# Expert look-ups of a PEER layer summed along contiguous positions, with wide products for every u item

## Chip, core and metric

One core of a Trainium2 chip runs the whole program in one launch. The metric is the device time of a launch in microseconds. TensorE is called PE here, VectorE DVE, ScalarE ACT, GpSimd POOL and SyncE SP, as in the profile.

## What is computed

256 tokens of width 1024 pass through two residual layers. Layer 0 mixes with a gated causal convolution, layer 1 with causal attention of 16 heads (256 tokens are one MoBA block, so it is plain causal attention). Each is followed by a PEER expert mixer, which is most of the work:

```python
q = (xc @ w_q).reshape(PEER_CHUNK, PEER_HEADS, 2, PEER_HALF)
s1 = jnp.einsum('thd,nd->thn', q[:, :, 0], sub_k1)      # 128 keys per half
s2 = jnp.einsum('thd,nd->thn', q[:, :, 1], sub_k2)
v1, i1 = lax.top_k(s1, 16); v2, i2 = lax.top_k(s2, 16)
cand = v1[..., :, None] + v2[..., None, :]              # 16 x 16 sums
cidx = i1[..., :, None] * 128 + i2[..., None, :]
top_s, top_pos = lax.top_k(cand, 16)
e_idx = jnp.take_along_axis(cidx, top_pos, axis=-1)     # the look-up
g = jax.nn.softmax(top_s, axis=-1)
a = jax.nn.gelu(jnp.einsum('td,thkd->thk', xc, u_emb[e_idx]))
out = jnp.einsum('thk,thkd->td', g * a, v_emb[e_idx])
```

There are 8 heads and 128 x 128 experts a layer.

## The kernel before, in words

**No gather.** The kernel multiplies all tokens with all 16384 rows of u and of v. The activations of all experts for all tokens lie in one large tensor, `big`, and those experts that a token did not choose are made zero by a product with one-hot rows. So a PEER layer is a u stage (128 items of 128 experts, 512 KB each), in which `A[:, k]` (a part of `big`) gets the gelu of item k, and a v stage of 128 items.

**Two parts of each number.** Every matrix is split into an upper part HI (fp32r) and the rest LO = value - HI, and a product is upper x upper + upper x lower + lower x upper. For an item of u the chain is: SP's queue loads RAW; DVE transposes RAW into TR (line 157); ACT writes HI (line 171); POOL writes LO in two halves (line 176); PE multiplies. Each of these has three buffers. `next_item` (line 221) puts the instructions of an item into every engine's queue in this order: the transposes for three items ahead, the splits for two ahead, the matmuls, then side work, then what was left for last.

**Narrow and wide products of u.** `products` calls `upper` for the eight 128-row blocks and then `lower` for the eight. `u_bank(k)` decides the form. The first 16 items of a layer (WIDE = 16) are narrow: a PSUM region of 256 columns, into which `upper` puts two matmuls of 256 columns (lines 967 and 968) and `lower` one (line 971). Gelu then reads two such items from the bank (line 1126). The later ones are wide: one matmul of 512 columns in `upper` (line 965), for the token's upper and lower parts side by side, so that a bank of 512 columns holds one item, and its two halves still have to be added. After each odd item ACT copies the second halves of two banks to A (line 1144), DVE adds the first halves (`both`, line 1134), and two items later ACT takes the gelu in place. Four banks serve in turn, so the matmuls of a pair of items wait for the addition of the pair before the last one.

**Side work.** Everything else of the layer (scores, top 16, look-ups, one-hot rows) goes into a queue `side` as pieces with a cost in microseconds, written by hand. `run_side` is called after the matmuls of each item with a budget (1.62 for an item of u); it issues pieces in order while their costs fit the credit, and a `pause` ends the item's share and sets the credit to zero. Pieces issued through `add` carry line 215 in the profile, those of `words` line 1020, of `fold` line 1029. DVE works through its queue in order; transposes, side pieces and additions stand in one line.

**The look-up.** For each half of the tokens (i = 0, 1) the top 16 of 65 candidate sums give positions, of which four bits name an entry of the second list and a table of steps the entry of the first. `hits` are one-hot rows, 16 heads-and-sides x 16 positions x 16 picks in float16, laid out with positions outside and picks inside; they are multiplied with the values (each value twice in the bank, so that pairs can be read), and then summed over positions with three folds (halves of the tile added to each other, both operands in SBUF) and a last addition. The subtraction of the largest score, `gg = ts - ts[0]`, is an operation with both operands in SBUF too. The bank `hi4[3]` holds picks, values and small intermediate numbers.

**The stage before.** In the attention layer `attn_mixer` multiplies the items of q, k and v; lower parts of some of these are POOL's (`on_pool`), in one instruction unless the item is in `halved`. The first two items of v are multiplied together by `next_group`, a bank at a time (lines 565 to 567).

Of the kernel before, what the change touches and what calls it, by code (L numbers as in the profile page):

```python
# [12 lines left out]
F16 = mybir.dt.float16  # L13
BF16 = mybir.dt.bfloat16
I32 = mybir.dt.int32
U32 = mybir.dt.uint32
AF = mybir.ActivationFunctionType
# [16 lines left out]
WIDE = (16, 16)  # L34
# [4 lines left out]
def trunk_kernel(ctx: ExitStack, tc, x, norm_mix, norm_ffn, conv_w_in, conv_w, conv_w_out,  # L39
# [43 lines left out]
    def scratch(off, n):  # L83
        return big[:, off:off + n]
# [610 lines left out]
    def attn_mixer():  # L695
# [131 lines left out]
        for g, banks in ((0, lo4), (1, hi4), (2, lo4)):  # L827
            n = state["use"] - 3 * (g == 0)
            if g == 0:
                on_pool.update(range(n + 15, n + 20))  # L830
                hi_dve.update(range(n + 21, n + 26))
# [75 lines left out]
    def peer(l):  # L907
# [4 lines left out]
        vp = [xbuf[:, 256 * i:256 * i + 256].bitcast(F16).rearrange("p (g a r) -> p g a r", a=16, r=2) for i in range(2)]  # L912
        hot = [scratch(base + 2048 * i, 2048).bitcast(F16).rearrange("p (g a n) -> p g a n", a=16, n=16)
               for i in range(2)]
# [8 lines left out]
        pf = scratch(o + 2176, 128).bitcast(F16).rearrange("p (s h n) -> p s h n", s=2, h=8)  # L923
# [5 lines left out]
        picks = hi4[3][:, 0:128].bitcast(F16).rearrange("p (s h n) -> p s h n", s=2, h=8)  # L929
        values = hi4[3][:, 128:384].bitcast(F16).rearrange("p (g a r) -> p g a r", a=16, r=2)  # L930
# [3 lines left out]
        io16 = scratch(o + 3280, 128).bitcast(F16).rearrange("p (a n) -> p a n", a=16)  # L934
        st16 = scratch(o + 3408, 128).bitcast(F16).rearrange("p (a n) -> p a n", a=16)
# [10 lines left out]
        pool.iota(io16, pattern=[[1, 16], [0, 16]], base=0, channel_multiplier=0,  # L946
                  allow_small_or_imprecise_dtypes=True)
        for a0, n, first, width in ((0, 1, 0, 0), (1, 2, 16, 8), (3, 4, 32, 4), (7, 9, 48, 2)):
            pool.iota(st16[:, a0:a0 + n], pattern=[[width, n], [0, 16]], base=first, channel_multiplier=0,
                      allow_small_or_imprecise_dtypes=True)  # L950
# [71 lines left out]
        def tables(i):  # L1022

            act.activation(vp[i][:, 0:8, 0], if16[:, i, 0, :, 0:1].to_broadcast([128, 8, 2]), AF.Copy)
            act.activation(vp[i][:, 8:16], if16[:, i, 1, :, :, None].to_broadcast([128, 8, 16, 2]), AF.Copy)

        def fold(i, n):
            v = hot[i].rearrange("p g a n -> p g (a n)")
            dve.tensor_tensor(v[:, :, 0:16 * n], v[:, :, 0:16 * n], v[:, :, 16 * n:32 * n], op=OP.add)
# [20 lines left out]
        for i in range(2):  # L1050
            add(0.4, words, room(0, 256), i16[:, i].rearrange("p s h n -> p (s h n)"))
            add(0.3, dve.tensor_copy, if16[:, i].rearrange("p s h n -> p (s h n)"), room(0, 256))
            add(0.4, dve.tensor_tensor, vp[i][:, 0:8, 1:16], if16[:, i, 0, :, 1:16, None].to_broadcast([128, 8, 15, 2]),
                if16[:, i, 0, :, 0:15, None].to_broadcast([128, 8, 15, 2]), op=OP.subtract)
# [10 lines left out]
            add(0.5, dve.tensor_tensor, gg[:, i], ts[:, i], ts[:, i, :, 0:1].to_broadcast([128, 8, 16]),  # L1065
# [7 lines left out]
            add(0.3, dve.tensor_copy, pf.rearrange("p s h n -> p (s h n)"), room(128, 256))  # L1073
            if i:
                add(0.0, act.activation, gg, gg, AF.Exp)
            add(0.3, words, hi4[3][:, 0:128].bitcast(U32), pf.rearrange("p s h n -> p (s h n)").bitcast(U32))
            add(0.4, words, hi4[3][:, 128:384].bitcast(U32), vp[i].rearrange("p g a r -> p (g a r)").bitcast(U32))
            add(1.4, dve.tensor_tensor, hot[i][:, 0:8], picks[:, 0, :, None, :].to_broadcast([128, 8, 16, 16]),
# [6 lines left out]
            for n in (8, 4, 2):  # L1085
                add(0.3 + 0.14 * n, fold, i, n)
# [260 lines left out]
```

## Time and profile before

| | |
|---|---|
| median of 3 runs | 1809.76 us (1808.52 to 1813.9) |
| the profiled execution | 1812.88 us, of which the span is 1811.1 us |
| PE busy | 99% of the span |
| DVE, ACT, POOL busy | 76%, 50%, 39% |
| DMA | 321 MB, 177 GB/s |
| mean granted clock of PE | 0.995 |

The profile is of one execution; the span runs from the first to the last instruction of the program, and the time of the execution is a little longer. Times in rows are in microseconds from the span's start. A row of the timeline has the start, the length, the engine, the line, the operation, output <- inputs, shapes and a count of merged instructions; a bracket holds the idle time before it and what ended it. Consecutive matmuls overlap in these rows, so a period is read from one start to the next. Within layer 0 the u stage lies from about 139 to 500 us, within layer 1 from about 1049 us on; the look-ups of layer 0 lie between 226 and 320 us.

### The profile page before, as it was taken

To read this page: it belongs to the slowest core of one execution; us is meant where nothing else is said; L and a number is where in the kernel's file an instruction comes from. 1 tells how busy PE (TensorE), PEld (TensorE's weight loads), DVE (VectorE), ACT (ScalarE), POOL (GpSimd) and SP (SyncE) were. 2 spreads that over 40 slices of the span, in tenths; PEclk is the share of its full clock that TensorE was granted. 3 is DMA by queue.
4 is the path that set the end of the run, shared out by engine and by line. 5 is a ranking of instruction groups with operands and counts; after the bars stand their busy time and mean duration, and the time that the engine had idled before them with its cause. 6 is when DMAs were issued, how large, how long until landed. Compare 5 with 4: busy or idle time off the path is not lost.

```text
span 1811.1 us, 30954 instructions
## 1 busy us (share of the span) xinstructions
PE 1791.1 (99%) x11217; PEld 1536.6 (85%) x11217; DVE 1370.7 (76%) x2251; ACT 906.8 (50%) x1153; POOL 700.2 (39%) x553
## 2 busy tenths in 40 slices
PE   9999999999999999999999999999999999999998
PEld 8979988888888888888878799888888888888886
DVE  4648899888888887555566488998888898875555
ACT  5455555554554444544454555565455544445443
POOL 1047888888720000000220388988888200000000
PEclk9999999999999999999999999999999999999999
DMA  7566566656556556766562665665565565657664
GB/s 206 157 196 197 167 176 174 187 166 176 171 157 182 168 171 185 228 193 196 172 181 83 174 198 168 182 179 174 172 175 164 158 186 169 176 176 230 193 193 138
DMA packets 204576, 321.06 MB, mean 177 GB/s; under 512 B 26221, under 2 KB 157317, under 8 KB 203910
## 3 DMA queue, kind: packets, MB, share of 16 engines
q1 hardware_dynamic: 202006, 312.33, 58.4%
q10 hardware_dynamic: 2416, 6.75, 1.1%
q8 instruction: 88, 1.44, 0.3%
q14 instruction: 66, 0.54, 0.1%
HBM read 315.83 MB, written 3.15 MB: 176 GB/s over the span
## 4 chain that ended last, share of the span: by engine, by line
PE 87%; DVE 7%; DMA 3%; issue 1%; ACT 1%; POOL 1%; SPq 1%; DVEq 0%; ACTq 0%; POOLq 0%
PE psum L558 40%; PE psum L965 19%; PE psum L971 11%; PE psum L1189 4%; PE psum L545 3%; DVE tr L157 2%; DVE big L215 2%; PE psum L968 2%; PE psum L967 2%; PE psum L591 2%; DMA raw<-in_peer_u_dram 1%; DVE lo L176 1%; PE psum L1003 1%; POOL lo L176 1%; PE psum L567 1%
## 5 line engine op out<-in xcount | busy, mean ns | idle before, releaser
L176 POOL TENSOR_TENSOR lo<-tr,hi 128x512 fp32r<-128x512 f32 x496 | 632.5, 1310 | 120.1 <-ACT hi L171 120.1
L171 ACT ACTIVATE hi<-raw 128x1024 fp32r<-128x1024 f32 x331 | 350.0, 1060 | 452.4 <-PE psum L558 362.7
L176 DVE TENSOR_TENSOR lo<-raw,hi 128x1024 fp32r<-128x1024 f32 x312 | 382.7, 1228 | 253.6 <-ACT hi L171 247.4
L558 PE MATMUL psum<-hi,x 128*128 128x512 f32 x2208 | 553.2, 392 | 0.7 <-ACT hi L171 0.7
L558 PEld LDWEIGHTS psum<-hi,x 128*128 128x128 f32 x2208 | 409.0, 188 | 82.6 <-ACT hi L171 1.1
L965 PE MATMUL psum<-x,hi 128*128 128x512 f32 x1792 | 458.9, 397 | 5.2 <-DVE big L1134 5.2
L965 PEld LDWEIGHTS psum<-x,hi 128*128 128x128 f32 x1792 | 323.2, 190 | 64.6 <-issue 4.2
L157 DVE STREAM_TRANSPOSE tr<-raw 128x1024 f32<-128x1024 f32 x256 | 315.6, 1233 | 43.2 <-DMA raw<-in_peer_u_dram 26.6
L171 ACT ACTIVATE hi<-tr 128x1024 fp32r<-128x1024 f32 x256 | 270.7, 1059 | 144.5 <-DVE tr L157 134.1
L558 PE MATMUL psum<-lo,x 128*128 128x512 f32 x1104 | 295.1, 389 | 0.4 <-POOL lo L176 0.4
L971 PEld LDWEIGHTS psum<-x,lo 128*128 128x128 f32 x2048 | 279.5, 191 | 18.0 <-POOL lo L176 0.2
L176 POOL TENSOR_TENSOR lo<-raw,hi 128x1024 fp32r<-128x1024 f32 (+1 forms) x31 | 58.3, 1904 | 599.7 <-ACT hi L171 558.1
L971 PE MATMUL psum<-x,lo 128*128 128x256 f32 x2048 | 289.2, 283 | 0.0
L558 PEld LDWEIGHTS psum<-lo,x 128*128 128x128 f32 x1104 | 207.1, 188 | 43.8 <-POOL lo L176 0.8
L1144 ACT ACTIVATE big<-psum 128x512 f32<-128x512 f32 x112 | 66.8, 596 | 165.6 <-PE psum L971 165.4
L1289 POOL TENSOR_TENSOR big<-xbuf,big 128x256 f32<-128x256 f32 x2 | 1.4, 732 | 383.4 <-DVE rstd L348 383.4
L1134 DVE TENSOR_TENSOR big<-psum,big 128x512 f32<-128x512 f32 x112 | 77.2, 689 | 72.3 <-ACT big L1144 72.0
L1174 DVE TENSOR_TENSOR xbuf<-psum,eT 128x1536 f16<-128x1536 f16 x128 | 119.8, 936 | 10.2 <-PE psum L1189 10.2
L1196 DVE SCALAR_TENSOR_TENSOR big<-psum,big 128x512 f32<-128x512 f32 x128 | 86.5, 677 | 3.1 <-PE psum L1189 3.1
L1182 DVE TENSOR_TENSOR xbuf<-xbuf,psum 128x1024 f16<-128x1024 f16 x128 | 85.8, 671 | 1.3
L1189 PEld LDWEIGHTS <-xbuf 128*128 128x128 f16 x2048 | 68.5, 97 | 19.5 <-issue 15.7
L1189 PE MATMUL psum<-xbuf 128*128 128x64 f16 x2048 | 83.7, 193 | 0.0
(173 smaller groups left out, 1451.0 us busy)
## 6 DMA issues: line engine op xcount, KB each, us to landing
raw<-in_peer_u_dram SPq DMA_DIRECT2D x1024, 128.0 KB, 2.9
raw<-in_peer_v_dram SPq DMA_DIRECT2D x256, 512.0 KB, 3.7
raw<-in_conv_w_in_dram SPq DMA_DIRECT2D x96, 128.0 KB, 2.7
raw<-in_attn_w_qkv_dram SPq DMA_DIRECT2D x96, 128.0 KB, 2.6
raw<-in_peer_w_q_dram SPq DMA_DIRECT2D x64, 128.0 KB, 3.1
raw<-in_conv_w_out_dram SPq DMA_DIRECT2D x8, 512.0 KB, 3.9
raw<-in_attn_w_o_dram SPq DMA_DIRECT2D x8, 512.0 KB, 3.6
x_dram<-xbuf ACTq DMA_DIRECT2D x2, 1024.0 KB, 4.8
```

The lines of the kernel that those rows point to most:

```text
L157: dve.transpose(TR[m % 3].rearrange("p b (g i) -> p g b i", g=4), RAW[m % 3].rearrange("p (g m) -> p g m", m=256))
L171: act.activation(HI[m % 3], src, AF.Copy)
L176: eng.tensor_sub(LO[m % 3][:, c], src[:, c], HI[m % 3][:, c])
L558: pe.matmul(banks[j], x[:, j // 2 * 128:j // 2 * 128 + 128], w[:, j % 2 * 512:j % 2 * 512 + 512], start=(first and p == 0), stop=(last and ...
L965: pe.matmul(o, w, X2[:, b], start=(b == 0), stop=False, skip_group_check=True)
L971: pe.matmul(o[:, 0:256], lo[:, b * 128:b * 128 + 128], XH[:, b], start=False, stop=(b == 7), skip_group_check=(o.shape[-1] == 512))
L1134: dve.tensor_tensor(a, halves(k, 0), a, op=OP.add)
L1144: act.activation(A[:, k - 1:k + 1], halves(k, 1), AF.Copy)
L1174: dve.tensor_tensor(HOT[s % 2].rearrange("p b (r k) t -> p b r k t", r=3), numbers[:, None, None].to_broadcast([128, TOK // 2, 3, 64, 2]), ...
L1182: dve.tensor_tensor(OHG[s % 2], one_hot[:, None].to_broadcast([128, 2, TOK // 2, 64, 2]), gate_rows[:, s, :, :, None, :].to_broadcast([128 ...
L1189: pe.matmul(o, pairs[:, t // 2, :, t % 2], OHG[s % 2][:, a, t // 2, :, t % 2], start=(a == 0), stop=(a == 1))
L1196: dve.scalar_tensor_tensor(w, banks[s % 3].rearrange("p (t k) -> p k t", k=64), 1.0 / GSC, w, op0=OP.mult, op1=OP.mult)
```

## The change

- `WIDE` goes from 16 to 0 in both layers: all u items are wide.
- The hits are laid out with picks outside and positions inside, so that the sum over the 16 positions runs along contiguous elements; two `tensor_reduce` replace the three folds and the closing addition. Picks lie in the bank twice (pairs), values once.
- The position numbers (`numb`) and the scores for the subtraction are first copied into the bank, so that no operation of the look-up has two operands in SBUF.
- The constant tables are 16 numbers each instead of 256; the table copies are smaller.
- A `pause` goes ahead of the sum of the gates, and some costs are written anew.
- The lower parts of the first two items of v are written in two halves.

```diff
@@ -31,7 +31,7 @@
 NEG = -1.0e30
 TOK = 8
 WARM = 22
-WIDE = (16, 16)
+WIDE = (0, 0)
 HEADS = ((0, 0), (0, 1), (1, 0), (0, 2), (0, 3), (1, 1), (1, 2), (1, 3))
 
 
@@ -828,6 +828,7 @@
             n = state["use"] - 3 * (g == 0)
             if g == 0:
                 on_pool.update(range(n + 15, n + 20))
+                halved.update((n + 16, n + 17))
                 hi_dve.update(range(n + 21, n + 26))
             if g:
                 next_group(qkv_first(banks), None, 2.5 * (g == 1))
@@ -909,8 +910,8 @@
         S = scratch(base, 4096).rearrange("p (b h s n) -> p b h s n", b=2, h=8, s=2)
         qT = scratch(80 * 256, 2048).rearrange("p (h t) -> p h t", t=256)
         qs = scratch(60 * 256, 1024).rearrange("p (t c) -> p t c", t=2)
-        vp = [xbuf[:, 256 * i:256 * i + 256].bitcast(F16).rearrange("p (g a r) -> p g a r", a=16, r=2) for i in range(2)]
-        hot = [scratch(base + 2048 * i, 2048).bitcast(F16).rearrange("p (g a n) -> p g a n", a=16, n=16)
+        vp = [xbuf[:, 128 * i:128 * i + 128].bitcast(F16).rearrange("p (g a) -> p g a", a=16) for i in range(2)]
+        hot = [scratch(base + 2048 * i, 2048).bitcast(F16).rearrange("p (g n a) -> p g n a", a=16, n=16)
                for i in range(2)]
         o = base + 4096
         cand = scratch(o, 8 * 66).rearrange("p (h c) -> p h c", c=66)
@@ -920,19 +921,19 @@
         if16 = scratch(o + 1024, 256).bitcast(F16).rearrange("p (b s h n) -> p b s h n", b=2, h=8, s=2)
         ts = scratch(o + 1280, 256).rearrange("p (b h n) -> p b h n", b=2, h=8)
         tp = scratch(o + 1536, 512).bitcast(U32).rearrange("p (b s h n) -> p b s h n", b=2, s=2, h=8)
-        pf = scratch(o + 2176, 128).bitcast(F16).rearrange("p (s h n) -> p s h n", s=2, h=8)
+        pf = scratch(o + 2048, 256).bitcast(F16).rearrange("p (m r) -> p m r", r=2)
         f15 = scratch(o + 2368, 128).bitcast(U32).rearrange("p (h n) -> p h n", h=8)
         e12 = scratch(o + 2496, 512).rearrange("p (b s n) -> p b s n", b=2, s=2)
         gg = scratch(o + 3008, 256).rearrange("p (b h n) -> p b h n", b=2, h=8)
         gs = scratch(o + 3264, 16).rearrange("p (b h) -> p b h", b=2)
 
-        picks = hi4[3][:, 0:128].bitcast(F16).rearrange("p (s h n) -> p s h n", s=2, h=8)
-        values = hi4[3][:, 128:384].bitcast(F16).rearrange("p (g a r) -> p g a r", a=16, r=2)
+        picks = hi4[3][:, 0:256].bitcast(F16).rearrange("p (s m r) -> p s m r", s=2, r=2)
+        values = hi4[3][:, 256:384].bitcast(F16).rearrange("p (g a) -> p g a", a=16)
         side1 = hi4[3][:, 384:512].rearrange("p (h n) -> p h n", h=8)
         room = lambda a, n: hi4[3][:, a:a + n].bitcast(U32)
         gr = hi4[3][:, 384:400].rearrange("p (b h) -> p b h", b=2)
-        io16 = scratch(o + 3280, 128).bitcast(F16).rearrange("p (a n) -> p a n", a=16)
-        st16 = scratch(o + 3408, 128).bitcast(F16).rearrange("p (a n) -> p a n", a=16)
+        io16 = scratch(o + 3280, 8).bitcast(F16)
+        st16 = scratch(o + 3408, 8).bitcast(F16)
         kbd = scratch(o + 3536, 256)
         kk = scratch(28416, 128)
 
@@ -943,10 +944,9 @@
         V0 = U0 + NK
         on_dve.update(range(V0 - 4, V0))
         act.dma_start(x_dram, xo)
-        pool.iota(io16, pattern=[[1, 16], [0, 16]], base=0, channel_multiplier=0,
-                  allow_small_or_imprecise_dtypes=True)
-        for a0, n, first, width in ((0, 1, 0, 0), (1, 2, 16, 8), (3, 4, 32, 4), (7, 9, 48, 2)):
-            pool.iota(st16[:, a0:a0 + n], pattern=[[width, n], [0, 16]], base=first, channel_multiplier=0,
+        pool.iota(io16, pattern=[[1, 16]], base=0, channel_multiplier=0, allow_small_or_imprecise_dtypes=True)
+        for a0, n, first, width in ((0, 1, 0, 1), (1, 2, 16, 8), (3, 4, 32, 4), (7, 9, 48, 2)):
+            pool.iota(st16[:, a0:a0 + n], pattern=[[width, n]], base=first, channel_multiplier=0,
                       allow_small_or_imprecise_dtypes=True)
         pool.iota(f15, pattern=[[0, 8], [0, 16]], base=15, channel_multiplier=0)
         pool.memset(kbd, 0.0)
@@ -1021,12 +1021,14 @@
 
         def tables(i):
 
-            act.activation(vp[i][:, 0:8, 0], if16[:, i, 0, :, 0:1].to_broadcast([128, 8, 2]), AF.Copy)
-            act.activation(vp[i][:, 8:16], if16[:, i, 1, :, :, None].to_broadcast([128, 8, 16, 2]), AF.Copy)
-
-        def fold(i, n):
-            v = hot[i].rearrange("p g a n -> p g (a n)")
-            dve.tensor_tensor(v[:, :, 0:16 * n], v[:, :, 0:16 * n], v[:, :, 16 * n:32 * n], op=OP.add)
+            act.activation(vp[i][:, 0:8, 0:1], if16[:, i, 0, :, 0:1], AF.Copy)
+            act.activation(vp[i][:, 8:16], if16[:, i, 1], AF.Copy)
+
+        def hits(i, c, ends, op):
+
+            dve.tensor_tensor(hot[i][:, 8 * c:8 * c + 8].rearrange("p h n (a r) -> p (h n) a r", r=2),
+                              picks[:, c, :, None].to_broadcast([128, 128, 8, 2]),
+                              ends.rearrange("p (a r) -> p a r", r=2)[:, None].to_broadcast([128, 128, 8, 2]), op=op)
 
         def ask(h):
             for i in range(2):
@@ -1048,10 +1050,10 @@
                 q_turn(0)
         q_out(1)
         for i in range(2):
-            add(0.4, words, room(0, 256), i16[:, i].rearrange("p s h n -> p (s h n)"))
-            add(0.3, dve.tensor_copy, if16[:, i].rearrange("p s h n -> p (s h n)"), room(0, 256))
-            add(0.4, dve.tensor_tensor, vp[i][:, 0:8, 1:16], if16[:, i, 0, :, 1:16, None].to_broadcast([128, 8, 15, 2]),
-                if16[:, i, 0, :, 0:15, None].to_broadcast([128, 8, 15, 2]), op=OP.subtract)
+            numb = hi4[3][:, 0:256].rearrange("p (s h n) -> p s h n", s=2, h=8)
+            add(0.4, dve.tensor_copy, numb, i16[:, i])
+            add(0.3, dve.tensor_copy, if16[:, i], numb)
+            add(0.4, dve.tensor_tensor, vp[i][:, 0:8, 1:16], numb[:, 0, :, 1:16], if16[:, i, 0, :, 0:15], op=OP.subtract)
             add(0.3, dve.tensor_copy, side1, v16[:, i, :, 1])
             for a0, n, first, width in ((0, 1, 0, 16), (1, 2, 16, 8), (3, 4, 32, 4), (7, 8, 48, 2), (15, 1, 64, 1)):
                 add(0.4, dve.tensor_tensor,
@@ -1062,7 +1064,8 @@
                 topk([(cand[:, h + a, 0:65], ts[:, i, h + a], tp[:, i, 0, h + a]) for a in range(4)], 0.25)
                 if h == 0:
                     add(0.0, tables, i)
-            add(0.5, dve.tensor_tensor, gg[:, i], ts[:, i], ts[:, i, :, 0:1].to_broadcast([128, 8, 16]),
+            add(0.3, dve.tensor_copy, side1, ts[:, i])
+            add(0.3, dve.tensor_tensor, gg[:, i], side1, ts[:, i, :, 0:1].to_broadcast([128, 8, 16]),
                 op=OP.subtract)
             top = tp[:, i, 0].rearrange("p h n -> p (h n)")
             add(0.3, words, room(128, 128), top)
@@ -1070,22 +1073,18 @@
             add(0.3, dve.tensor_tensor, room(0, 128), f15.rearrange("p h n -> p (h n)"), room(0, 128),
                 op=OP.logical_shift_right)
             add(0.3, dve.tensor_tensor, room(256, 128), top, room(0, 128), op=OP.bitwise_and)
-            add(0.3, dve.tensor_copy, pf.rearrange("p s h n -> p (s h n)"), room(128, 256))
+            add(0.6, dve.tensor_copy, pf, room(128, 256)[:, :, None].to_broadcast([128, 256, 2]))
             if i:
                 add(0.0, act.activation, gg, gg, AF.Exp)
-            add(0.3, words, hi4[3][:, 0:128].bitcast(U32), pf.rearrange("p s h n -> p (s h n)").bitcast(U32))
-            add(0.4, words, hi4[3][:, 128:384].bitcast(U32), vp[i].rearrange("p g a r -> p (g a r)").bitcast(U32))
-            add(1.4, dve.tensor_tensor, hot[i][:, 0:8], picks[:, 0, :, None, :].to_broadcast([128, 8, 16, 16]),
-                st16[:, None].to_broadcast([128, 8, 16, 16]), op=OP.is_ge)
-            add(1.4, dve.tensor_tensor, hot[i][:, 8:16], picks[:, 1, :, None, :].to_broadcast([128, 8, 16, 16]),
-                io16[:, None].to_broadcast([128, 8, 16, 16]), op=OP.is_equal)
-            pairs = hot[i].rearrange("p g a (n r) -> p g a n r", r=2)
-            add(2.5, dve.tensor_tensor, pairs, pairs, values[:, :, :, None, :].to_broadcast([128, 16, 16, 8, 2]),
-                op=OP.mult)
-            for n in (8, 4, 2):
-                add(0.3 + 0.14 * n, fold, i, n)
-            add(0.6, dve.tensor_tensor, e12[:, i].rearrange("p s (h n) -> p (s h) n", h=8), hot[i][:, :, 0],
-                hot[i][:, :, 1], op=OP.add)
+            add(0.4, words, room(0, 256), pf.rearrange("p m r -> p (m r)").bitcast(U32))
+            add(0.3, words, room(256, 128), vp[i].rearrange("p g a -> p (g a)").bitcast(U32))
+            add(1.2, hits, i, 0, st16, OP.is_ge)
+            add(1.2, hits, i, 1, io16, OP.is_equal)
+            add(2.3, dve.tensor_tensor, hot[i], hot[i], values[:, :, None].to_broadcast([128, 16, 16, 16]), op=OP.mult)
+            for c in range(2):
+                add(1.7, dve.tensor_reduce, e12[:, i, c].rearrange("p (h n) -> p h n", h=8),
+                    hot[i][:, 8 * c:8 * c + 8], axis=AX.X, op=OP.add)
+        pause()
         add(0.8, dve.tensor_reduce, gs, gg, axis=AX.X, op=OP.add)
         add(0.2, dve.reciprocal, gr, gs)
         add(0.8, dve.tensor_tensor, gg, gg, gr[:, :, :, None].to_broadcast([128, 2, 8, 16]), op=OP.mult)
```

## Rows read from the trace of the kernel before

**Rows 1.** The page: busy time of each engine, and two of its costliest groups.
```profile
PE 1791.1 (99%) x11217; PEld 1536.6 (85%) x11217; DVE 1370.7 (76%) x2251; ACT 906.8 (50%) x1153; POOL 700.2 (39%) x553
...
L176 POOL TENSOR_TENSOR lo<-tr,hi 128x512 fp32r<-128x512 f32 x496 | 632.5, 1310 | 120.1 <-ACT hi L171 120.1
...
L1174 DVE TENSOR_TENSOR xbuf<-psum,eT 128x1536 f16<-128x1536 f16 x128 | 119.8, 936 | 10.2 <-PE psum L1189 10.2
```

**Rows 2.** Waits of PE: total us, times, the longest us.
```profile
PE psum L965 <- DVE big L1134: 5.2, 4, 1.9
```

**Rows 3.** Timeline of PE: first matmuls of two narrow items, then of two wide ones.
```profile
145.67 0.28 PE L967 MATMUL psum<-x,hi 128*128 128x256 f32 x1
...
148.55 0.28 PE L967 MATMUL psum<-x,hi 128*128 128x256 f32 x1
...
281.61 2.00 PE L965 MATMUL psum<-x,hi 128*128 128x512 f32 x8
...
284.40 2.00 PE L965 MATMUL psum<-x,hi 128*128 128x512 f32 x8
```

**Rows 4.** Timeline of PE: u items around the waits, layer 0, then layer 1.
```profile
292.78 2.00 PE L965 MATMUL psum<-x,hi 128*128 128x512 f32 x8
...
296.42 2.08 PE L965 MATMUL psum<-x,hi 128*128 128x512 f32 x8 [0.69 <-DVE big L1134]
...
315.82 3.62 PE L965 MATMUL psum<-x,hi 128*128 128x512 f32 x8 [1.91 <-DVE big L1134]
...
320.23 2.00 PE L965 MATMUL psum<-x,hi 128*128 128x512 f32 x8
...
1225.91 2.73 PE L965 MATMUL psum<-x,hi 128*128 128x512 f32 x8 [1.92 <-DVE big L1134]
```

**Rows 5.** Windows: stretch, us, then busy time of each engine, clock, DMA.
```profile
138.90:189.30 50.40, 50.40 (x409) 49.93 (x408) 42.10 (x168) 25.27 (x31) 41.09 (x34) 1.00 0.64 189
...
190.00:230.00 40.00, 40.00 (x230) 35.13 (x229) 36.13 (x128) 22.30 (x29) 36.09 (x29) 1.00 0.58 170
...
315.80:319.30 3.50, 3.48 (x9) 2.77 (x10) 3.46 (x7) 2.32 (x4) 1.63 (x2) 0.52 0.37 105
```

**Rows 6.** Timeline of DVE in the look-ups of layer 0.
```profile
262.39 2.06 DVE L1029 TENSOR_TENSOR big<-big 128x2048 f16<-128x2048 f16 x1
...
271.80 0.68 DVE L1134 TENSOR_TENSOR big<-psum,big 128x512 f32<-128x512 f32 x1
...
290.93 4.22 DVE L215 TENSOR_TENSOR big<-big 128x128 f32<-128x128 f32 x1
...
295.60 0.68 DVE L1134 TENSOR_TENSOR big<-psum,big 128x512 f32<-128x512 f32 x1
...
310.50 4.57 DVE L1029 TENSOR_TENSOR big<-big 128x2048 f16<-128x2048 f16 x3
315.00 0.68 DVE L1134 TENSOR_TENSOR big<-psum,big 128x512 f32<-128x512 f32 x1
```

**Rows 7.** DVE's groups from 226 to 324 us: count | busy us, mean ns | idle.
```profile
L157 DVE STREAM_TRANSPOSE tr<-raw 128x1024 f32<-128x1024 f32 x33 | 40.7, 1234 | 0.5 <-DMA raw<-in_peer_u_dram 0.5
L1134 DVE TENSOR_TENSOR big<-psum,big 128x512 f32<-128x512 f32 x17 | 11.6, 684 | 3.0 <-ACT big L1144 3.0
...
L215 DVE TENSOR_TENSOR big<-psum,big 128x2048 f16<-128x2048 f16 x4 | 4.7, 1184 | 0.0
L215 DVE TENSOR_TENSOR big<-big,psum 128x4096 f16<-128x4096 f16 x2 | 4.5, 2249 | 0.0
...
L215 DVE TENSOR_TENSOR big<-big,psum 128x128 f32<-128x128 f32 x8 | 1.8, 271 | 0.0
...
L215 DVE TENSOR_REDUCE big<-big 128x16 f32<-128x256 f32 x1 | 0.4, 402 | 0.0
```

**Rows 8.** Timeline around the first two items of v: POOL and PE.
```profile
941.51 4.73 POOL L176 TENSOR_TENSOR lo<-raw,hi 128x1024 fp32r<-128x1024 f32 x2 [1.27 <-ACT hi L171]
...
943.93 0.50 PE L567 MATMUL psum<-lo,x 128*128 128x512 f32 x1 [1.72 <-POOL lo L176]
```

## The prediction

> **What bounds the kernel now.** I read the page's busy times first: TensorE (PE) is busy for 1791.1 us of a span of 1811.1 us [rows 1], so little can be won but what PE waits for, what it does slowly, and the instructions that it need not issue. Then the waits of PE: the largest by far is for line 1134, the DVE addition that empties two PSUM banks of the u stage, 5.2 us in 4 waits [rows 2]. The timeline of PE shows where: two waits in the u stage of each layer, of 0.69 and 1.91 us in layer 0 and as long in layer 1 [rows 4]. After the second wait eight matmuls take 3.62 us where they take 2.00 elsewhere [rows 3, 4], and the granted clock over these 3.5 us is 0.52 [rows 5], so the lower level (1.2 GHz) for nearly all of them: PE had idled for 1.9 us just before. A u item has a period of 2.79 us (281.61 to 284.40) where the products are wide, and of 2.88 us (145.67 to 148.55) in the first 16 items, where they are narrow [rows 3]. From 292.78 to 320.23 lie eight items; 27.45 us less 8 x 2.79 is 5.13 us lost [rows 4]. That is the waits, the slow clock and about 0.9 us of small slips.
>
> Why the addition is late stands in the DVE timeline [rows 6]. Ahead of the first late addition (295.60) lies a subtraction of 128 elements that took 4.22 us; ahead of the second (315.00) lie three folds, 4.57 us together. An operation on 128 elements with one operand in PSUM takes 0.27 us [rows 7]. GpSimd (POOL) meanwhile works nearly without a pause: two lower parts of 1.31 us an item [rows 1], 2.62 of 2.79 us. I read the 4.22 us as a wait for POOL, by an operation that has both operands in SBUF.
>
> The Trainium skill, "SBUF — State Buffer", section "Who interferes with whom", says that a DVE instruction with two SBUF inputs contends with a GpSimd instruction that reads SBUF and that the second one to issue blocks in full, while one with at most one SBUF input, outside the two-port modes, does not contend. By that rule the subtraction costs what rows 7 show for 128 elements; if instead it were slow by itself, the waits would stay, and that is rival 3.
>
> **The change part by part.**
>
> 1. *All u products wide.* Items 0 to 15 of each layer change from 24 matmuls to 16: 2.88 - 2.79 = 0.09 us each, 32 items, **2.9 us**, on PE and so on the path. It adds to DVE, in each layer, 8 of the additions of line 1134 at 0.684 us [rows 7], 5.5 us, and to ACT 8 copies. What hides them: in this stretch ACT is busy 25.27 and DVE 42.10 of 50.40 us [rows 5], so 8.3 us of DVE are idle; with the additions it has 47.6 us of work against 49.0 us that PE will need. Behind an addition in DVE's queue stand the next transpose and the top-16 search; the next pair of items but one waits for the addition. The same mixture (wide products, top-16 searches) already runs from 190 to 230 us: DVE busy 36.13 of 40 us, PE all 40.00 [rows 5]. Bounds: nothing, or all 8.3 us of idle stay idle (47.6 + 8.3 - 49.0 = 6.9 us a layer). I take nothing, because the nearest stretch shows it.
>
> 2. *Subtraction of the largest score.* A copy to the bank and a subtraction with a bank operand, both near 0.27 us, instead of 4.22 us in the second list [rows 6, 7]. **DVE is 3.7 us earlier there.**
>
> 3. *Picks.* The pairs copy writes 512 elements (nearest row: line 1134 with 512, 0.684 us) where it wrote 256: 0.27 us more by the slope in step 5. The words of the picks double, those of the values halve. Together about +0.3 us a list. The first steps (numbers held in the bank) come out even. Table copies on ACT and iotas on POOL shrink; neither is waited for.
>
> 4. *Hits and product.* Same element counts: 2 x 1.184 and 2.249 us [rows 7]. The hits now walk in pairs with one operand repeated; line 1174 does that with 1536 elements in 0.936 us [rows 1], the same rate. So I take no change; the other end, one element at a time, is worked out under rival 2.
>
> 5. *Folds against two sums.* Three folds (4.57 us in list two) and the closing pair addition go; two reductions of 2048 elements come. No row has that. Low end: 1.184 us, the hits' pace. High end: the 0.402 us of a reduction of 256 elements times eight, 3.22 us. I take 2.33: 0.402 plus 1792 elements at (1.234 - 0.684) / 512 = 1.07 ns, the slope between 512 and 1024 elements on DVE [rows 7].
>
> The Trainium skill, "VectorE: DVE Perf Modes", section "Rules for kernel authors", speaks against this step: expect one element at a time from a reduction, the slowest operation of the engine, and restructure. By the page's clock of 0.96 GHz 2048 elements are an estimated 2.1 us plus the start, so it excludes the low end and agrees with 2.33; its warning holds for folds that are not held up, and here they are [rows 6].
>
> 6. *One pause more, other costs.* Adding up the planner's costs against its 1.62 an item: the lists come one item later (after 64 items, not 63), the one-hot products of the first half end at item 124 instead of 123 of 127, before the last item would have to drain them. Price: nothing. More useful: at most one reduction goes into one item, where three folds went into one.
>
> 7. *v's lower parts halved.* PE waits 1.72 us at 943.93 for the second v item's lower part, which POOL began at 941.51 and which takes 2.4 us (4.73 for two) [rows 8]. In halves of 1.31 us the first is there at 942.82, **1.1 us** earlier; the second, at 944.1, is wanted six matmuls after PE starts again, some 1.4 us (an item of 2.79 us holds eight of these and eight of half the width), so in time. POOL's next item comes 0.2 us later, and PE first has the rest of this group to do.
>
> **Do the waits go?** The addition that started at 295.60 let PE start 0.85 us late (295.57, which is 292.78 + 2.79, became 296.42), so its deadline was 294.75; those of the other pairs lie 2 x 2.79 = 5.58 us apart. In the second list DVE is free at 290.93. Four small operations put the first addition at 292.05 (deadline 294.75). From there each pair costs DVE two transposes at some 1.16 us (they overlap a little), the addition at 0.6, and its share of the list: 297.9 (300.3), then with a hit and the product 304.1 (305.9), one reduction 309.3 (311.5), the other and the closing sums 315.2 (317.1). The least spare time is 1.8 us. In the first list a reduction stands where a fold began at 262.39; the addition behind it comes at 264.7 (deadline 266.85), the next, after another reduction and five small steps (1.6 us), at 271.5 (272.43; before it was 271.80, and PE did not wait). Spare 0.9 us. So both waits go, and with no idle PE before it the slow clock goes too: **5.1 us a layer, 10.2 us**; layer 1 is taken like layer 0. Late next is POOL, with 0.17 us to spare an item; it falls behind only if a transpose is late, and DVE's lag shrinks.
>
> Sum: 2.9 + 10.2 + 1.1 = 14.2 us. The profiled execution took 1812.88 us (span 1811.1): 1798.7 after. The median shown, 1809.76, is 3.1 us below it, with runs from 1808.52 to 1813.9; 14.2 off it is 1795.6. If the faster runs were those in which the clock did not fall (2 x 1.6 us), they have less to gain, if they differ by something else, as much. I put the forecast between: **1797.2 us**.
>
> **Rivals.**
>
> Rival 1, *the reductions are long*: at 3.22 us the second addition of the first list starts at 273.2, 0.8 us past its deadline; with a fall of the clock behind it (1.6 us) that is 2.4 a layer, 1802.0 us. For: no row of this size. Against: the slope, and that the wait of 0.69 us drew no slow clock (the item after it took 2.08 us).
>
> Rival 2, *slower than before*: the pair form loses double rate, hits 2.3 us each, product 4.4. First list: the addition after the product starts 2.3 us past its deadline, the next another 1.3; second list: 2.6. With a slow stretch of 1.6 us after each: 11 us a layer, 22 us, 1819.2 us. It decides from a product of about 4 us on. Against: line 1174 [rows 1].
>
> Rival 3, *the bank does not help*: DVE's small operations still wait 4 us for POOL; only 2.9 + 1.1 us are won, 1797.2 + 10.2 = 1807.4 us, no measurable change. For: only one such operation shows the extreme. Against: operations with a bank operand show steady times [rows 7].
>
> Rival 4, *the first 16 items become DVE's*: up to 6.9 us a layer, 1811 us at worst; half of that, 1804, is likelier. Against: rows 5.
>
> **How the numbers follow.** The forecast has 0.74, rival 1 0.11, rival 2 0.04, rival 3 0.05, rival 4 0.06. A difference of under 0.3% (5.4 us, about the spread of the runs shown) can hardly be told from none: faster means under 1804.3, slower over 1815.2. The forecast and rival 1 are faster, as is a piece of rival 4: 0.86. Rival 3 and the rest of 4: 0.10. Rival 2: 0.04. The range reaches down to 1792.5 (3 us of scatter below the median's own 1795.6) and up to 1803.5, which takes in rival 1 and leaves out rivals 2, 3 and most of 4.
>
> **What would show it.** Right: no wait of PE for line 1134, granted clock 1.0 through both u stages, 2.79 us an item from the first on, the subtraction under 0.3 us, reductions near 2.3 us, PE's wait at the second v item under 0.7 us. Wrong: an addition of line 1134 that PE still waits for, a product over 4 us, items over 2.85 us among the first 16, or a new wait of PE for POOL's lower parts.

## The result, and the profile after

The changed kernel takes 1799.12 us (median of 4 runs, 1798.38 to 1800.45) against 1810.51 us before (4 runs beside it, 1808.52 to 1813.9); the ratio is 0.9937, 95% interval 0.9922 to 0.9952. The forecast was 1797.2, range 1792.5 to 1803.5. The profiled execution took 1800.45 us, span 1798.7 us, 12.4 us less than the span before.

The page's busy times, to be read against [rows 1]:

```profile
PE 1784.0 (99%) x10961; PEld 1520.2 (85%) x10961; DVE 1371.4 (76%) x2263; ACT 914.5 (51%) x1169; POOL 694.0 (39%) x555
```

PE issues 256 matmuls fewer (16 items x 2 layers x 8) and is busy 7.1 us less; DVE's total is the same. The waits of PE, largest first, against [rows 2]:

```profile
PE psum L299 <- DVE ident L291: 1.4, 1, 1.4
PE psum L372 <- DVE big L367: 1.3, 3, 0.5
PE psum L567 <- DVE lo L176: 1.0, 4, 0.4
...
PE psum L567 <- POOL lo L176: 0.6, 1, 0.6
```

No wait for the addition (line 1133 now) is left; what remains are small waits of the stages between and of the start. One of them is new against the profile before: line 567, in the attention layer, waits for lower parts that DVE writes (1.0 us in all). The timeline of PE in the first items, against [rows 3]:

```profile
142.97 2.09 PE L965 MATMUL psum<-x,hi 128*128 128x512 f32 x8
144.91 1.11 PE L971 MATMUL psum<-x,lo 128*128 128x256 f32 x8
145.85 2.00 PE L965 MATMUL psum<-x,hi 128*128 128x512 f32 x8
147.69 1.11 PE L971 MATMUL psum<-x,lo 128*128 128x256 f32 x8
148.65 2.00 PE L965 MATMUL psum<-x,hi 128*128 128x512 f32 x8
```

145.85 to 148.65 is 2.80 us, where an item took 2.88. The windows, against [rows 5]: the first 16 items, and both stretches of the look-ups (layer 0, layer 1).

```profile
138.90:187.90 49.00, 49.00 (x279) 43.12 (x279) 44.07 (x166) 29.05 (x39) 40.87 (x33) 1.00 0.61 181
...
225.00:324.00 99.00, 99.00 (x570) 87.19 (x569) 93.20 (x230) 59.98 (x85) 87.81 (x71) 1.00 0.66 189
1135.00:1232.00 97.00, 97.00 (x559) 85.40 (x558) 91.35 (x213) 59.15 (x84) 86.32 (x69) 1.00 0.64 187
```

PE is busy for all of each, at a granted clock of 1.00. DVE's timeline in the second list of layer 0, against [rows 6]:

```profile
289.19 0.28 DVE L215 COPY psum<-big 128x128 f32<-128x128 f32 x1
289.50 0.29 DVE L215 TENSOR_TENSOR big<-psum,big 128x128 f32<-128x128 f32 x1
...
290.37 0.68 DVE L1133 TENSOR_TENSOR big<-psum,big 128x512 f32<-128x512 f32 x1
...
296.42 0.68 DVE L1133 TENSOR_TENSOR big<-psum,big 128x512 f32<-128x512 f32 x1
...
302.60 0.68 DVE L1133 TENSOR_TENSOR big<-psum,big 128x512 f32<-128x512 f32 x1
...
304.35 2.24 DVE L215 TENSOR_REDUCE big<-big 128x128 f32<-128x2048 f16 x1
...
307.67 0.65 DVE L1133 TENSOR_TENSOR big<-psum,big 128x512 f32<-128x512 f32 x1
```

Copy and subtraction take 0.57 us together in place of 4.22, and a reduction 2.24 us. Its groups from 222 to 324 us, against [rows 7]:

```profile
L215 DVE TENSOR_REDUCE big<-big 128x128 f32<-128x2048 f16 x4 | 9.0, 2240 | 0.0
...
L1029 DVE TENSOR_TENSOR big<-psum,big 128x2048 f16<-128x2048 f16 x4 | 4.8, 1194 | 0.0
L215 DVE TENSOR_TENSOR big<-big,psum 128x4096 f16<-128x4096 f16 x2 | 4.5, 2247 | 0.0
...
L215 DVE CAST big<-psum 128x512 f16<-128x512 uint32 x2 | 1.4, 690 | 0.1
```

And the first two items of v, against [rows 8]: POOL's two halves (the row merges them with the undivided lower part behind them), and PE's wait of 0.64 us where it was 1.72.

```profile
936.20 4.90 POOL L176 TENSOR_TENSOR lo<-raw,hi 128x512 fp32r<-128x512 f32 x3 [1.14 <-ACT hi L171]
...
937.55 0.50 PE L567 MATMUL psum<-lo,x 128*128 128x512 f32 x1 [0.64 <-POOL lo L176]
```

**Where the 12.4 us are.** I take the start of the first matmul of items 0, 16, 52, 64 and 127 of each u stage from the timelines of PE and subtract, for this and all the profiles below (us; layer 0 / layer 1). The last column is from item 127 of layer 0 to item 0 of layer 1, with layer 0's v stage and the attention layer in it.

| kernel | items 0 to 16 | 16 to 52 | 52 to 64 | 64 to 127 | between the layers |
|---|---|---|---|---|---|
| before | 50.37 / 50.38 | 100.56 / 100.56 | 39.27 / 39.33 | 194.33 / 194.33 | 525.50 |
| changed | 48.97 / 48.97 | 100.56 / 100.56 | 34.17 / 34.19 | 194.33 / 194.33 | 525.77 |
| before, again | 50.38 / 50.37 | 100.56 / 100.56 | 37.73 / 37.75 | 194.33 / 194.33 | 525.55 |
| changed, again | 48.97 / 48.97 | 100.56 / 100.56 | 34.17 / 34.19 | 194.33 / 194.33 | 525.73 |
| subtraction alone | 50.38 / 50.37 | 100.56 / 100.56 | 34.19 / 34.17 | 194.33 / 194.33 | 526.03 |
| two-operand subtraction | 48.97 / 48.97 | 100.56 / 100.56 | 37.38 / 34.17 | 194.33 / 194.33 | 524.75 |
| the same, again | 48.97 / 48.96 | 100.56 / 100.56 | 37.38 / 34.17 | 194.33 / 194.33 | 525.80 |
| narrow | 50.38 / 50.37 | 100.56 / 100.56 | 34.17 / 34.17 | 194.33 / 194.33 | 524.61 |
| without the new sums | 48.97 / 48.97 | 100.56 / 100.56 | 34.17 / 34.17 | 194.33 / 194.33 | 526.08 |

Between before and changed: 2 x 1.4 us in the first items, 5.1 + 5.1 in the look-ups. To these comes +0.4 before the first u item (139.06 became 139.41) and +0.3 between the layers, although 1.1 us are won there at v's first items. Both stretches scatter: over these nine profiles the first u item starts between 137.79 and 139.70 us, and the last column spans 1.5 us.

### The profile page after: what moved, and what is told of

Same layout as the page of the kernel before. It is cut to its first block, busy times and chain, and to the rows that moved or that the text cites. A ratio compares the mean times of both kernels' runs of the same rounds, so it can differ in the third digit from the quotient of the medians.

```text
span 1798.7 us, 30479 instructions
## 1 busy us (share of the span) xinstructions
PE 1784.0 (99%) x10961; PEld 1520.2 (85%) x10961; DVE 1371.4 (76%) x2263; ACT 914.5 (51%) x1169; POOL 694.0 (39%) x555
## 3 DMA queue, kind: packets, MB, share of 16 engines
q8 instruction: 86, 1.41, 0.3%
## 4 chain that ended last, share of the span: by engine, by line
PE 92%; DMA 3%; DVE 2%; ACT 1%; POOL 1%; issue 1%; SPq 0%; DVEq 0%; ACTq 0%; POOLq 0%
PE psum L558 39%; PE psum L965 26%; PE psum L971 14%; PE psum L1188 4%; PE psum L545 3%; PE psum L591 2%; DVE lo L176 1%; PE psum L1003 1%; POOL lo L176 1%; DMA raw<-in_conv_w_out_dram 1%; ACT hi L171 1%; DMA raw<-in_attn_w_qkv_dram 0%; PE psum L567 0%; PE psum L771 0%; PE psum L598 0%
## 5 line engine op out<-in xcount | busy, mean ns | idle before, releaser
L965 PE MATMUL psum<-x,hi 128*128 128x512 f32 x2048 | 521.3, 396 | 0.0
L965 PEld LDWEIGHTS psum<-x,hi 128*128 128x128 f32 x2048 | 368.3, 189 | 66.6
L176 POOL TENSOR_TENSOR lo<-raw,hi 128x512 fp32r<-128x512 f32 (+1 forms) x33 | 58.6, 1801 | 601.1 <-ACT hi L171 558.7
L1143 ACT ACTIVATE big<-psum 128x512 f32<-128x512 f32 x128 | 76.4, 597 | 177.3 <-PE psum L971 177.1
L1133 DVE TENSOR_TENSOR big<-psum,big 128x512 f32<-128x512 f32 x128 | 88.0, 688 | 75.0 <-ACT big L1143 74.3
L1173 DVE TENSOR_TENSOR xbuf<-psum,eT 128x1536 f16<-128x1536 f16 x128 | 119.8, 936 | 10.2 <-PE psum L1188 10.2
```

The costliest lines, as they stand in the source:

```text
L176: eng.tensor_sub(LO[m % 3][:, c], src[:, c], HI[m % 3][:, c])
L965: pe.matmul(o, w, X2[:, b], start=(b == 0), stop=False, skip_group_check=True)
L1133: dve.tensor_tensor(a, halves(k, 0), a, op=OP.add)
L1143: act.activation(A[:, k - 1:k + 1], halves(k, 1), AF.Copy)
L1173: dve.tensor_tensor(HOT[s % 2].rearrange("p b (r k) t -> p b r k t", r=3), numbers[:, None, None].to_broadcast([128, TOK // 2, 3, 64, 2]), ...
```

## The experiments

**The subtraction alone.** The kernel before with one edit:

```diff
-            add(0.5, dve.tensor_tensor, gg[:, i], ts[:, i], ts[:, i, :, 0:1].to_broadcast([128, 8, 16]),
+            add(0.3, dve.tensor_copy, side1, ts[:, i])
+            add(0.3, dve.tensor_tensor, gg[:, i], side1, ts[:, i, :, 0:1].to_broadcast([128, 8, 16]),
```

> The kernel before, with the subtraction of the largest score alone changed (scores first copied to the bank). My theory: DVE is 3.7 us earlier in the second list, and both waits hang on that. The first wait of PE for line 1134 (0.69 us) goes. The addition behind the three folds comes at about 311.6 against a deadline of 311.5, so the second wait falls from 1.9 us to 0 to 0.3 us, and the slow clock behind it goes too: 4.2 to 5.1 us a layer, 8.5 to 10 us in all, about 1801 us. Rival, each wait has its own cause: the second wait (1.9 us) and the slow clock (1.6 us) stay, because three folds of 4.6 us still stand ahead of the addition; only some 0.9 us a layer is won, about 1808.5 us.

Measured: 1801.98 us (10 runs) against 1809.81 before, beside it, ratio 0.9961 (0.9949 to 0.9973). Both waits are gone in both layers, with the folds still there: 34.19 / 34.17 us from item 52 to 64. DVE's timeline in the second list:

```profile
288.80 0.28 DVE L215 COPY psum<-big 128x128 f32<-128x128 f32 x1
289.12 0.29 DVE L215 TENSOR_TENSOR big<-psum,big 128x128 f32<-128x128 f32 x1
...
305.91 3.73 DVE L1029 TENSOR_TENSOR big<-big 128x2048 f16<-128x2048 f16 x2
309.56 0.68 DVE L1135 TENSOR_TENSOR big<-psum,big 128x512 f32<-128x512 f32 x1
...
311.32 0.38 DVE L1029 TENSOR_TENSOR big<-big 128x512 f16<-128x512 f16 x1
```

The folds come as two and one, 4.1 us in all, and PE does not wait. The edit also changed the costs of the pieces, and with them moved the last fold behind the addition; that is not what saves PE. With that fold (0.38 us here; 0.84 by 4.57 less 3.73) ahead of it the addition would have started by 310.4, by my estimate, against a deadline of 310.31 (the item at 311.16 less 0.85): at most 0.1 us late, where PE had waited 1.91. So the second wait was the first one's consequence: DVE had no time in hand when it came to the folds. My theory holds, the rival falls. This one edit carries all that the look-ups gain, 5.1 us a layer against the first profile of before. The median moved by 7.8 us and not by 10.2; the second profile of before, below, shows why.

Is it the bank operand, or only that the subtraction now stands elsewhere? In the eight profiles of kernels with the copy there are 32 such subtractions, which meet POOL's instructions at different moments, 28 of them beside a working POOL. Each took 0.29 us, so it is the operand.

**The sums with the old subtraction.** The changed kernel with that edit undone:

```diff
-            add(0.3, dve.tensor_copy, side1, ts[:, i])
-            add(0.3, dve.tensor_tensor, gg[:, i], side1, ts[:, i, :, 0:1].to_broadcast([128, 8, 16]),
+            add(0.5, dve.tensor_tensor, gg[:, i], ts[:, i], ts[:, i, :, 0:1].to_broadcast([128, 8, 16]),
```

> The changed kernel, with the subtraction again on two SBUF operands. My theory: it takes about 4 us in the second list again, the addition behind it is some 0.9 us late, and with no time in hand the next two additions are late by 0.3 to 0.6 us; 1.8 us a layer, 3 to 5 us in all, about 1803 us, mostly without a slow clock. Rival, the sums are what matters: the reductions give DVE enough time, PE waits at most once and 0.7 us a layer, about 1800.5 us or less.

Measured: 1801.97 us (10 runs), ratio 0.9959 (0.9945 to 0.9972), but not as either theory had it. In layer 0 the subtraction took 4.57 us and PE waited 0.61 and 1.41 us, 3.2 us lost in all; in layer 1 it took 0.82 us and nothing was lost. The timeline of PE in layer 0:

```profile
294.29 2.06 PE L965 MATMUL psum<-x,hi 128*128 128x512 f32 x8 [0.61 <-DVE big L1132]
...
313.42 2.06 PE L965 MATMUL psum<-x,hi 128*128 128x512 f32 x8 [1.41 <-DVE big L1132]
```

With the reductions in place a long subtraction still brings two waits, so they do not replace the other edit; and how long it takes depends, as I read it, on how it meets POOL. A second profile was to tell whether that is chance:

> The changed kernel with the subtraction on two SBUF operands, once more and unchanged, for a second profile: in the first one the second list's subtraction took 4.57 us in layer 0 and 0.82 us in layer 1. If how it meets POOL's instructions is chance, layer and length will differ this time; if the order of the program fixes it, it is 4.6 and 0.8 us again, and 37.4 and 34.2 us from item 52 to 64.

It is not chance, as far as two profiles can tell: 37.38 / 34.17 us again (1803.48 us, one run), and the same lengths. DVE's timeline of that second profile, layer 0 and layer 1:

```profile
288.94 4.57 DVE L215 TENSOR_TENSOR big<-big 128x128 f32<-128x128 f32 x1
...
1195.99 0.81 DVE L215 TENSOR_TENSOR big<-big 128x128 f32<-128x128 f32 x1
```

**Narrow products again.** The changed kernel with the old constant:

```diff
-WIDE = (0, 0)
+WIDE = (16, 16)
```

> The changed kernel with the first 16 items narrow again. My theory: 2.88 us an item again, item 16 of each layer comes 1.4 us later against item 0, the rest is as in the changed kernel; 2.8 us more in all, about 1802 us. Rival, the additions for these items cost DVE time that the look-ups miss later: part of the 1.4 us comes back by item 70, under 2 us in all.

Measured: 1801.5 us (9 runs) against 1809.81 beside it, ratio 0.9956 (0.9943 to 0.9968). 50.38 / 50.37 us for the first 16 items and every later stretch as in the changed kernel: 1.4 us a layer, nothing of it given back.

**Three parts without the new sums.** The subtraction's edit, the constant and the halves of v, put into the kernel before:

```diff
-WIDE = (16, 16)
+WIDE = (0, 0)
...
+                halved.update((n + 16, n + 17))
```

> The kernel before with three of the four parts: the subtraction through the bank, all u products wide, the two items of v halved; picks, folds and tables stay as they were. My theory, the new sums bring no time to PE's path: 48.97 us for items 0 to 15, 34.2 us from item 52 to 64 in both layers, 1799 us like the changed kernel. Rival, with the wide products the additions leave no time in hand in the first list, where the folds had 0.6 us: PE waits there for 0.3 to 1 us a layer, 1800 to 1801 us.

Measured: 1799.41 us (4 runs) against 1810.89 before, beside it, ratio 0.9927 (0.9909 to 0.9946), and each u stretch equal to the changed kernel's within 0.02 us (that kernel, beside it, took 1799.91 us). The new picks, sums and tables bring PE nothing here; they cost it nothing either. The rival's wait in the first list did not come.

**Both kernels once more.**

> The kernel before once more, unchanged, for a second profile. If the two waits of PE hang on how the subtraction meets POOL's instructions, which may differ from one execution to the next, then the stretch from item 52 to 64 can be anything from 34.2 to 39.3 us, and may differ between the layers. If they are fixed by the order of the program, it is 39.3 us in both layers again.

> The changed kernel once more, unchanged, beside the others on one chip: 34.2 us from item 52 to 64 in both layers, 1799 us, 2 us less than with the subtraction alone (1802) or with narrow products (1801.5).

The changed kernel: 1799.91 us (4 runs), ratio 0.9933 (0.9914 to 0.9952), 34.17 / 34.19 us again. The kernel before: 1808.54 us in this one run. The subtraction took 4.24 us in both layers and PE waited 0.69 and 1.91 us, as in the first profile; yet the look-ups cost 37.73 / 37.75 us, 1.6 us a layer less. The matmuls after the second wait, against [rows 4], and the window of 3.5 us there, against the last of [rows 5], show why:

```profile
314.57 2.06 PE L965 MATMUL psum<-x,hi 128*128 128x512 f32 x8 [1.91 <-DVE big L1134]
```

```profile
314.50:318.00 3.50, 3.43 (x19) 3.05 (x20) 3.47 (x7) 2.27 (x4) 1.63 (x2) 1.00 0.33 98
```

The granted clock stayed at 1.00 (2.4 GHz) after the same wait, where it was 0.52 in the first profile. The order of the program fixes the waits, not the fall of the clock. My expectation had 39.3 us or something between the extremes by way of the waits; it was the clock. Of the 4.3 us between the two profiles 3.1 are this, and 1.3 lie before the first u item.

**Is it POOL?** The changed kernel with idle subtractions of 128 elements, both operands in SBUF:

```diff
+                if 4 <= k < 20:
+                    dve.tensor_tensor(gg[:, 0].rearrange("p h n -> p (h n)"), ident, ident, op=OP.subtract)
...
+                if 90 <= k < 106:
+                    dve.tensor_tensor(TR[0][:, 0], ident, ident, op=OP.subtract)
```

> The changed kernel with 32 more subtractions a layer of 128 elements, both operands in SBUF: 16 in items 4 to 19 of the u stage, where POOL writes lower parts nearly without a pause, and 16 in items 90 to 105 of the v stage, where POOL does nothing. They compute nothing that is used. My theory, the operation waits for POOL: 0.3 us each in the v stage, in the u stage between 0.3 and 4.3 us, over 1 us in the mean. Rival, such an operation is slow by itself: the same mean in both. Rival, POOL has nothing to do with it and only the second list's was held up by something of its own: 0.3 us in both. The time of the whole is not what is looked at; the added work in the u stage will make PE wait.

The groups of DVE for the two places (u stage, then v stage):

```profile
L1150 DVE TENSOR_TENSOR big<-ident 128x128 f32<-128x128 f32 x32 | 18.4, 576 | 0.0
...
L1248 DVE TENSOR_TENSOR tr<-ident 128x128 f32<-128x128 f32 x32 | 9.1, 284 | 0.0
```

In the v stage, with POOL idle, all 32 took 0.28 us. In the u stage they took 0.24 to 1.31 us, and each longer one ended some 0.15 us after the end of a POOL instruction. So the operation is not slow by itself; it waits for POOL. But the mean, 0.58 us, is well under what I expected, and none came near 4 us. Nor did the added work make PE wait, as I had expected: the run took 1799.17 us, and its list of waits has no addition.

**How does it come to 4.2 us?** The same in items 20 to 61, which was to meet POOL with more instructions ready in a row:

```diff
+                if 20 <= k < 62:
+                    dve.tensor_tensor(xbuf[:, 2048:2176], ident, ident, op=OP.subtract)
```

> The changed kernel with 42 more subtractions a layer of 128 elements, both operands in SBUF, one in each of the items 20 to 61 of the u stage; nothing uses them. There DVE is close to full, so transposes come late and then together, and POOL works through longer rows of ready instructions than in items 4 to 19. The question is how the subtraction of the kernel before came to 4.2 us, when a lower part of POOL takes 1.3 us. Theory A, it is let in at the end of the POOL instruction that it meets: nearly all under 1.5 us, hardly one of 84 over 2 us. Theory B, it can be passed over for as long as POOL has ready instructions: several over 2.5 us, each ending some 0.15 us after the end of a POOL instruction, the longest where POOL has three or more ready. PE will wait; the whole time is not looked at.

All 84 took under 1.4 us, 596 ns in the mean. That is theory A: each of these was let in at the latest at the end of the POOL instruction that it met. Then in the form of the look-up's own subtraction:

```diff
+        rows = ident.rearrange("p (h n) -> p h n", n=16)
...
+                if 20 <= k < 54:
+                    dve.tensor_tensor(e12[:, 1, 0].rearrange("p (h n) -> p h n", n=16), rows, rows[:, :, 0:1].to_broadcast([128, 8, 16]),
+                                      op=OP.subtract)
```

> The changed kernel with 34 more subtractions a layer in items 20 to 53 of the u stage, this time in the form of the one that took 4.2 us: 128 elements in 8 rows of 16, the second operand the first number of each row repeated, the output in the large tensor. Nothing uses them. Theory C, the form matters (a repeated operand is passed over by POOL): several of 68 over 2 us. Theory A, it does not: all under 1.5 us, as with the plain form, and why the look-up's own subtraction was passed over three times stays open. The whole time is not looked at.

Again none over 1.4 us; the groups of DVE in these two runs (1832.01 and 1829.16 us, as here the added work does make PE wait):

```profile
L1150 DVE TENSOR_TENSOR xbuf<-ident 128x128 f32<-128x128 f32 x84 | 50.1, 596 | 0.0
```

```profile
L1152 DVE TENSOR_TENSOR big<-ident 128x128 f32<-128x128 f32 x68 | 42.4, 624 | 0.0
```

The form alone does not do it. But the two runs did not make the rows of POOL that they were meant for: with the added subtractions POOL paused after every two to four instructions in this stretch (items 20 to 61 lie from 199 to 329 us in the run with 84). One such row from the run with 84, then POOL's timeline in the kernel before, and one in layer 1 of the second profile of the sums with the old subtraction:

```profile
283.96 5.11 POOL L176 TENSOR_TENSOR lo<-tr,hi 128x512 fp32r<-128x512 f32 x4 [1.42 <-ACT hi L171]
```

```profile
274.89 20.11 POOL L176 TENSOR_TENSOR lo<-tr,hi 128x512 fp32r<-128x512 f32 x16 [0.65 <-ACT hi L171]
298.68 2.55 POOL L176 TENSOR_TENSOR lo<-tr,hi 128x512 fp32r<-128x512 f32 x2 [3.68 <-ACT hi L171]
```

```profile
1180.27 20.18 POOL L176 TENSOR_TENSOR lo<-tr,hi 128x512 fp32r<-128x512 f32 x16 [0.97 <-ACT hi L171]
```

In the kernel before POOL worked through sixteen instructions without a pause, until 295.00; the subtraction began at 290.93 and ended at 295.15, 0.15 us after the last of them. It was passed over at the ends of three POOL instructions, which none of the 184 idle subtractions was in the u stage (32, 84 and 68), and it got in where POOL had nothing more to do: POOL's next instruction came after 3.68 us of idle time. So it is in all six of the long ones (two in each profile of the kernel before, one in each with the sums and the old subtraction). A long row of POOL does not settle it either, for the subtraction of 0.81 us at 1195.99 was let in at the first end, in the middle of sixteen. Why it is passed over at one place and not at another stays open.

## Why the prediction was right

**The waits (10.2 us).** Right in place and cause, and in size for the profiled execution: 5.1 us a layer, clock 1.00; in the second profile of before there were only 3.6 us a layer to win. The deadlines held too: with 0.28 and 0.29 us for the copy and the subtraction the additions of the second list came before PE wanted them. Where I was off is the share of the parts: I counted the folds as the cause of the second wait. The run with the subtraction alone shows that they were late only because the subtraction had used up DVE's time in hand.

**Wide products (2.9 us).** Right: 2 x 1.4 us. DVE was busy 44.07 of 49.00 us there, under the 47.6 that I allowed for, and PE never waited. Rival 4 is out.

**Sums (no time of their own).** The reduction was taken as 2.33 us and is 2.24, so rival 1 with 3.22 is out. The Trainium skill, "VectorE: DVE Perf Modes", section "Rules for kernel authors", says to expect a reduction at one element at a time and to consider restructuring. 2.24 us for 2048 elements agrees with the first; the second costs nothing here, since two of 2.24 us stand where 4.57 us of folds and the closing addition stood. That this part brings nothing, I had not said: it hides in time that DVE has in hand once the subtraction is short.

**Hits, product, picks.** 1.194 and 2.247 us against 1.184 and 2.249, so rival 2 is out; the copy of pairs 0.690 us, as taken from line 1134.

**The bank.** Rival 3 is out: 0.28 and 0.29 us. The Trainium skill, "SBUF — State Buffer", section "Who interferes with whom", says that a DVE instruction with two SBUF inputs contends with a POOL instruction that reads SBUF, and one with at most one, outside the two-port modes, does not. The traces agree in kind: 0.28 us with POOL idle, up to 1.4 us with POOL at work, and 0.29 us with one operand in PSUM. They go beyond it in the 4.2 us, the wait through four POOL instructions in a row.

**v in halves (1.1 us).** From the second group of transposes of line 750 to the third, around v's first two items, it is 11.12 us in the kernel before (937.30 to 948.42) and 11.07 with the subtraction alone, 10.03 in the changed kernel: 1.1 us at its place. In the whole it is not shown. From item 127 of layer 0 to the second of these groups it is 413.71 to 413.76 us in the three profiles without the halves and 413.81 to 414.93 in the six with them: up to 1.2 us are lost there, in PE's waits for DVE's lower parts at line 567, some 20 us ahead of the halves. In the changed kernel ACT waits 0.68 us for a load just before. Whether the halves have a part in these waits is open, as no run has them alone.

**The sum against the median.** The place is right and the forecast 1.9 us too low. 14.2 off 1812.88 gave 1798.7; that execution's counterpart took 1800.45, 12.4 us less, because the 0.4 us at the start and some 1.4 us between the layers (1.1 of them the term for v) came on top, both within the scatter of those stretches. Off the median I took 14.2 as well (1795.6), took as the other end a median without a fall of the clock (11.0 less, 1798.8), and put the forecast halfway. The second profile of before shows the other end: without the fall of the clock the look-ups lose 3.55 us a layer, not 5.1, so such an execution has 11 us to gain. The median moved by 11.4 us. Halfway was a guess: which of the runs behind the median had the fall of the clock is not on record, and the stretches that scatter do so by as much as the miss. That the forecast came within 2 us is in part luck.

## What to carry to other kernels

When PE waits for an engine that is busy all the time, look in that engine's queue for the one instruction that takes many times what its size asks for: a two-SBUF-operand operation of 128 elements on DVE beside a busy POOL took 4.22 us, where one with an operand in PSUM takes 0.29, and a copy of 0.28 us into PSUM removed it and both waits of PE. Test parts alone before crediting them: here a rewrite of the sums brought nothing that the copy had not already brought. And when several profiles of one kernel differ by a few microseconds, compare the granted clock after each wait before taking one of them as the base of a sum.

## What was not expected of the hardware

The same wait of PE of 1.91 us was followed by a granted clock of 0.52 over 3.5 us in one execution and of 1.00 in another (layer 0; in layer 1 the same idle was followed by 0.59 from 1226.5 to 1230.0 us in the one and 1.00 in the other); that is 1.6 us a layer. And a DVE operation with two SBUF operands, which in 184 trials in the u stage took at most 1.4 us, waited through four POOL instructions (4.2 to 4.6 us) at one place in the program, until POOL had nothing more to do, in each profile of the kernel before and, in one of the layers, of the one with the new sums.
